# A decoder layer on one core: the output projection accumulates in the attention's four PSUM banks

## The chip, the cores and the metric

The kernel runs on one core of a Trainium2 chip (the profile calls it core 0 of [0]). The metric is the device time of one execution in microseconds (us). Three runs of the kernel before took 2811.61, 2813.51 and 2815.99 us; the median is 2813.51 us. The profile is of one further execution, which took 2810.97 us, with a traced span of 2809.2 us.

The engines are named as the profile names them: PE is the matrix engine, PEld its weight loads, DVE, ACT and POOL the three engines for vectors and scalars, SP the engine that issues the DMA transfers. Each runs its own instructions strictly in their order and waits on semaphores for the others.

## What is computed

One layer on 4096 tokens of width 1024. The input is normalised and projected into eight groups of 512 columns. Half of the columns feed eight heads of a dilated sliding-window attention with three patterns (dilations 16, 4 and 1), the other half four heads of a gated linear recurrence (HGRN2). Each branch is normalised per head and gated; both are put side by side, projected, added to the input, and normalised:

```python
y_attn = _head_rmsnorm(attn, attn_out_norm_w[layer], ATTN_HEADS) * jax.nn.silu(ag.astype(f32))
y_hgrn = _head_rmsnorm(rec, hgrn_out_norm_w[layer], HGRN_HEADS) * jax.nn.silu(hg.astype(f32))
mixed = jnp.concatenate([y_attn, y_hgrn], axis=-1).astype(x.dtype)
x = x + mixed @ w_out[layer]
...
return _rmsnorm(x, final_norm_w)
```

The change concerns `mixed @ w_out`: a 4096x1024 matrix times a 1024x1024 one, in float32.

## The kernel before

**Three stages.** The first (to about 720 us of the trace) makes the attention's projections for 32 blocks of 128 rows; it has its own PSUM pools, five banks `m` among them. The second (about 730 to 2360 us) interleaves the projections and the recurrence of the HGRN2 heads with the attention, which is a generator that yields after each piece and is advanced between the recurrence's blocks. The third (from about 2366 us) is the output projection. It overlaps the last pieces of the attention, since what `take(10 ** 9)` leaves of the generator is issued ahead of it.

**PSUM in the second and third stage.** Eight banks of 128x512 float32: one `proj` (pool `ps_p`), four `att` (`ps_t`), one `po` (`ps_o`), and `hp1` and `hp2` (`ps_h`). A tile of a pool with one bank can be written only when whoever reads the tile before it is done. A pool with four banks hands them out in the order of the program, so that a new tile waits for the readers of the fourth last one.

**Who uses them.** `project_T` and `project_N` of the HGRN2 heads use `proj`. The attention uses `att` for scores (`score`, L419 and L420), for transposed weights (`flip`, L442), for maxima and sums, and in `finish` for four tiles of transposed outputs (L599 and L600), which DVE multiplies into `pr` (L602). The output projection, `project`, uses `proj` as well.

**The output projection, row by row.** A row is a block `b` of 128 tokens. `load_y(b)` reads its two halves from DRAM into `raw` (three buffers, L870), transposes each with four matmuls into `hp1` and `hp2` (L874), and splits them into a high and a low part `xs` (ACT L170, DVE L171; five buffers). `project` then does 24 matmuls of 128x512 for each half `n` of the output columns: eight steps `k` of three products high x high (L183), high x low (L184) and low x high (L185). `residual` adds the bank to the input row `xr` on DVE (L904) and so frees the bank. `final_norm` takes the squares on ACT (L911), some small operations on DVE and ACT, and a scaling of the row on DVE (L914); the row is then written (L915). In the loop, `load_y(b + 1)` stands ahead of the two projections of `b`. The first two rows are apart: both are projected on the first half of the weights before the second half has been split (`w1hi`, `w1lo`, L862 and L863, from the four buffers `woraw`, L858).

**What sets the order.** The framework's scheduler orders each engine's instructions by a simulated timeline, so that the order in the program is not the order of the code; but the banks of a pool go round in the order of the code.

Of the kernel before, what the change touches and what calls it, by code (L numbers as in the profile page):

```python
# [17 lines left out]
F32 = mybir.dt.float32  # L18
# [31 lines left out]
def layer(ctx: ExitStack, tc: tile.TileContext, x, xT, xP, pos, w_in, w_out, nw, anw, hnw, lbraw, fnw,  # L50
# [124 lines left out]
        return t[:, 0:512], t[:, 512:1024]  # L175

    def project(X, W):
        ps = ps_p.tile([128, 512], F32, name="proj")
        for k in range(KT):
            hi, lo = X[k // 4]  # L180
            c = slice((k % 4) * 128, (k % 4 + 1) * 128)
            whi, wlo = W[k]
            T.matmul(ps, hi[:, c], whi, start=(k == 0), stop=False)  # L183
            T.matmul(ps, hi[:, c], wlo, start=False, stop=False)  # L184
            T.matmul(ps, lo[:, c], whi, start=False, stop=(k == KT - 1))  # L185
        return ps
# [626 lines left out]
    ps_p = ctx.enter_context(tc.tile_pool(name="ps_p", bufs=1, space=PSUM))  # L813
    ps_t = ctx.enter_context(tc.tile_pool(name="ps_t", bufs=4, space=PSUM))
# [72 lines left out]
    take(10 ** 9)  # L887
    Y = [load_y(0), load_y(1)]
    ps0 = [project(Y[0], WO[0]), project(Y[1], WO[0])]
    w1hi = big.tile([128, S], F32R, name="w1hi", tag="QS")  # L890
    w1lo = big.tile([128, S], F32R, name="w1lo", tag="KH")
# [27 lines left out]
    for b in range(2):  # L919
        residual(b, 1, project(Y[b], WO[1]))  # L920
        final_norm(b)
    Yn = load_y(2)
    for b in range(2, NB):
        Yb, Yn = Yn, load_y(b + 1) if b + 1 < NB else None
        for n in range(2):
            residual(b, n, project(Yb, WO[n]))
        final_norm(b)
# [50 lines left out]
```

## Time and profile before

| | |
|---|---|
| median of three runs | 2813.51 us |
| profiled execution, its own time | 2810.97 us |
| its span in the trace | 2809.2 us |
| PE busy | 2609.6 us (93%) |
| DVE, ACT, POOL busy | 1949.5 us (69%), 1714.1 us (61%), 917.1 us (33%) |
| DMA moved | 475.90 MB, mean 169 GB/s |
| first matmul of the output projection | at 2366.17 us |
| first matmul of row 2, where the loop begins | at 2406.76 us |
| last matmul | begins at 2799.52 us |

In the timeline a row gives start, duration, engine, line, operation, output and inputs, the number of merged instructions, and in brackets how long the engine had been idle and what ended that. Matmuls overlap, so the step from one start to the next is the time that each takes of PE; the duration of one is longer. In the table of stretches (windows), each stretch has the busy time of the engines with the number of instructions, the clock granted to PE (1.00 is full speed), the DMA engines' busy share and their rate. In the list of waits, each row gives who waited for whom, the sum in us, how often, and the longest.

### The profile page before, as it was taken

The page shows a single profiled execution, that of the slowest core. Times are in us where ns is not written, and L with a number is a line of the kernel's source. Part 1 is how long each engine was busy: PE and PEld are TensorE (multiplying, and loading weights), DVE is VectorE, ACT ScalarE, POOL GpSimd, SP SyncE. Part 2 cuts the span into 40 slices and gives each one's busy share as a digit, 9 for nine tenths or more (in the row PEclk, how much of TensorE's full clock was granted, in tenths as well). Part 3 has the DMA queues.
Part 4 walks back from the last instruction along what each step waited for, and adds up shares of the span by engine and source line. Part 5 has one row for each costly group of instructions (what it writes and reads, how often), then busy time and mean ns, then how long its engine had stood idle before and what let it go on. Part 6 is the DMA issues. An engine that isn't in the chain of part 4 may idle for free.

```text
span 2809.2 us, 52085 instructions
## 1 busy us (share of the span) xinstructions
PE 2609.6 (93%) x17330; PEld 2337.8 (83%) x17330; DVE 1949.5 (69%) x5267; ACT 1714.1 (61%) x4847; POOL 917.1 (33%) x900
## 2 busy tenths in 40 slices
PE   6899989999879999999999999999999998999997
PEld 4678867888769898899999899999899998777776
DVE  8777788777556786886777876777877768533343
ACT  8755565555557687677677786687776776222221
POOL 5456546565423453331331321422312312100000
PEclk8999999999989999999999999999999999999999
DMA  6855464444865865865756746647647545434432
GB/s 231 254 172 152 140 189 143 143 147 135 247 174 182 239 202 165 241 172 149 197 152 178 230 124 191 182 145 215 192 128 221 155 136 171 143 117 122 122 117 64
DMA packets 452192, 475.90 MB, mean 169 GB/s; under 512 B 119336, under 2 KB 334420, under 8 KB 451924
## 3 DMA queue, kind: packets, MB, share of 16 engines
q1 hardware_dynamic: 451924, 472.58, 56.9%
q8 instruction: 138, 2.26, 0.3%
q14 instruction: 130, 1.06, 0.1%
HBM read 346.06 MB, written 126.37 MB: 168 GB/s over the span
## 4 chain that ended last, share of the span: by engine, by line
PE 69%; DVE 13%; DMA 9%; ACT 4%; issue 2%; SPq 2%; POOL 1%; DVEq 0%; POOLq 0%; ACTq 0%
PE proj L210 19%; PE m L721 6%; PE m L719 6%; PE m L720 6%; PE po L454 5%; PE proj L183 5%; PE att L442 4%; PE proj L185 4%; PE proj L184 4%; PE att L419 3%; PE att L420 3%; DVE xr L904 2%; DMA y_d<-pr 1%; DMA raw<-x 1%; DMA mr<-ml_d 1%
## 5 line engine op out<-in xcount | busy, mean ns | idle before, releaser
L210 PE MATMUL proj<-xs,whi 128*128 128x256 f32 x2048 | 430.9, 299 | 10.7 <-ACT hgv L344 5.8
L210 PE MATMUL proj<-whi,xs 128*128 128x256 f32 x2048 | 414.4, 291 | 16.0 <-DVE hz L317 15.7
L210 PEld LDWEIGHTS proj<-xs,whi 128*128 128x128 f32 x2048 | 336.8, 198 | 18.3 <-ACT hgv L344 8.0
L210 PEld LDWEIGHTS proj<-whi,xs 128*128 128x128 f32 x2048 | 330.4, 192 | 19.0 <-DVE hz L317 9.5
L430 DVE CUSTOM_DVE_ANT_0 pt<-att,mask 128x256 f32<-128x256 f32 (+1 forms) x768 | 269.1, 388 | 97.6 <-PE att L420 94.8
L210 PE MATMUL proj<-xs,wlo 128*128 128x256 f32 x1024 | 305.6, 298 | 4.5 <-DVE wlo L162 4.5
L210 PE MATMUL proj<-wlo,xs 128*128 128x256 f32 x1024 | 295.4, 289 | 0.0
L446 DVE TENSOR_TENSOR pl<-att,ph 128x512 fp32r<-128x512 f32 (+1 forms) x384 | 237.4, 625 | 64.8 <-ACT ph L445 62.6
L432 ACT ACTIVATE pt<-pt,ml 128x256 f32<-128x256 f32 (+1 forms) x512 | 238.3, 468 | 45.3 <-DVE ml L430 44.2
L445 ACT ACTIVATE ph<-att 128x512 fp32r<-128x512 f32 (+1 forms) x384 | 203.2, 544 | 80.5 <-PE att L442 44.7
L442 PE MATMUL att<-ident,pt 128*128 128x128 f32 x1368 | 228.6, 279 | 4.3 <-ACT pt L432 2.5
L454 PE MATMUL po<-ph,vh 128*128 128x128 f32 (+1 forms) x856 | 212.6, 279 | 11.0 <-ACT ph L445 4.4
L210 PEld LDWEIGHTS proj<-xs,wlo 128*128 128x128 f32 x1024 | 201.7, 197 | 9.4 <-DVE wlo L162 6.7
L454 PE MATMUL po<-pl,vh 128*128 128x128 f32 (+1 forms) x856 | 204.6, 285 | 3.7 <-DVE pl L446 3.7
L210 PEld LDWEIGHTS proj<-wlo,xs 128*128 128x128 f32 x1024 | 197.1, 192 | 0.0
L454 PEld LDWEIGHTS po<-ph,vh 128*128 128x128 f32 x856 | 164.6, 192 | 15.8 <-ACT ph L445 4.9
L442 PEld LDWEIGHTS att<-ident,pt 128*128 128x128 f32 x1368 | 161.9, 143 | 9.9 <-ACT pt L432 3.5
L719 PE MATMUL m<-tw,ss 128*128 128x512 f32 x384 | 154.6, 403 | 16.0 <-ACT tw L170 6.6
L454 PEld LDWEIGHTS po<-pl,vh 128*128 128x128 f32 x856 | 164.7, 192 | 5.7 <-DVE pl L446 4.9
L419 PE MATMUL att<-KH,qc 128*128 128x256 f32 (+1 forms) x512 | 144.2, 306 | 15.6 <-DMA vh<-v_d 14.1
L720 PE MATMUL m<-tw,ss 128*128 128x512 f32 x384 | 153.9, 401 | 4.9 <-DVE tw L171 4.9
L721 PE MATMUL m<-tw,ss 128*128 128x512 f32 x384 | 155.1, 404 | 0.0
(256 smaller groups left out, 7502.3 us busy)
## 6 DMA issues: line engine op xcount, KB each, us to landing
xs<-xh_d SPq DMA_DIRECT2D x192, 512.0 KB
xr<-xT SPq DMA_DIRECT2D x128, 256.0 KB
qk_d<-stk SPq DMA_DIRECT2D x128, 256.0 KB
xh_d<-xs SPq DMA_DIRECT2D x64, 512.0 KB
vh<-v_d SPq DMA_DIRECT2D x512, 64.0 KB
raw<-x SPq DMA_DIRECT2D x64, 256.0 KB
v_d<-hl SPq DMA_DIRECT2D x128, 128.0 KB
raw<-xP SPq DMA_DIRECT2D x64, 256.0 KB
```

The costliest lines, as they stand in the source:

```text
L183: T.matmul(ps, hi[:, c], whi, start=(k == 0), stop=False)
L210: m = T.matmul(o, l, r, start=first is None, stop=(k == KT - 1 and g == len(groups) - 1 and n == 2))
L419: T.matmul(o, q[:, j % 2 * 128 : (j % 2 + 1) * 128], cols(KH, *ks), start=True, stop=False)
L430: V.tensor_tensor_reduce(out=p_, in0=o, in1=mask[:, (1, 4, 16).index(d), 256 - 128 * nk : 256], scale=-0.125, scalar=3e38, op0=ALU.add, op ...
L432: A.activation(p_, p_, AF.Exp, scale=-1.0, bias=m, accum_out=l)
L442: T.transpose(ps[:, n * 128 : (n + 1) * 128], loc[u], ident)
L445: A.activation(ph[:, :w], ps[:, :w], AF.Copy)
L446: V.tensor_sub(pl[:, :w], ps[:, :w], ph[:, :w].bitcast(F32))
L454: T.matmul(po[:, 128 * c : 128 * (c + n)], v, rh, start=(s == 0), stop=(s == len(steps) - 1))
L719: T.matmul(ps, hi[:, c], whi, start=start and k == 0, stop=False, skip_group_check=not start)
L720: T.matmul(ps, hi[:, c], wlo, start=False, stop=False, skip_group_check=not start)
L721: T.matmul(ps, lo[:, c], whi, start=False, stop=(k == 3), skip_group_check=not start)
```

## The change

The output projection's accumulator is a tile of the pool `ps_t`, under the attention's name `att`, instead of a tile of `ps_p`. The projections of the HGRN2 heads stay in `proj`. No instruction is added or taken away and no tile changes its size.

```diff
     def project(X, W):
-        ps = ps_p.tile([128, 512], F32, name="proj")
+        ps = ps_t.tile([128, 512], F32, name="att")
         for k in range(KT):
             hi, lo = X[k // 4]
             c = slice((k % 4) * 128, (k % 4 + 1) * 128)
```

Up to the end of the second stage both programs are alike on all engines; POOL's order is the same throughout. After that the scheduler orders PE, ACT, DVE and SP anew. Three places are shown, with buffer numbers and with the semaphores that an instruction waits for.

**PE, in the loop over rows, between the two projections of one row.** Before (`proj_34864` is the first half of the columns, `proj_34891` the second; `hp1_35028` holds half of a later row):

```order
L185 MATMUL proj_34864<-whi_32231,xs_34770 128x512
L874 MATMUL hp1_35028<-ident_89,raw_35026 128x128 [waits DMAHW2_49,DVE_49,PE_49]
L874 MATMUL hp1_35028<-ident_89,raw_35026 128x128 x3
L183 MATMUL proj_34891<-w1hi_32339,xs_34760 128x512 [waits DVE_49]
L184 MATMUL proj_34891<-w1lo_32340,xs_34760 128x512
```

Now the same boundary:

```order
L184 MATMUL att_34864<-wlo_32232,xs_34770 128x512
L185 MATMUL att_34864<-whi_32231,xs_34770 128x512
L183 MATMUL att_34891<-w1hi_32339,xs_34760 128x512
L184 MATMUL att_34891<-w1lo_32340,xs_34760 128x512
L185 MATMUL att_34891<-w1hi_32339,xs_34760 128x512
```

The transposes are gone from between the two projections, and the second one begins without a wait for DVE. The eight transposes of a later row stand together at the end of the row, ahead of the next row's first projection:

```order
L185 MATMUL att_34891<-w1hi_32339,xs_34770 128x512
L874 MATMUL hp1_34937<-ident_89,raw_34935 128x128 [waits DMAHW0_49,DVE_49]
L874 MATMUL hp1_34937<-ident_89,raw_34935 128x128 x3
L874 MATMUL hp2_34947<-ident_89,raw_34945 128x128 [waits DMAHW3_49,DVE_49]
L874 MATMUL hp2_34947<-ident_89,raw_34945 128x128 x3
L183 MATMUL att_34955<-whi_32189,xs_34851 128x512 [waits Activation_49]
```

That projection waits for ACT's copy of its own row (`xs_34851`), whose transposes stand one row earlier; it too has no wait for DVE.

**PE, at the end of the attention, before `finish` of the last eight blocks.** Before, the first projection (`proj_32289`) stood among the attention's instructions, behind the first two L600 of the last `finish` but one (`att_30206` and `att_30211`):

```order
L600 MATMUL att_30206<-ident_89,o1_29977 128x2x64
L600 MATMUL att_30211<-ident_89,o1_29977 128x2x64
L183 MATMUL proj_32289<-whi_32189,xs_32256 128x512 [waits Activation_49]
L184 MATMUL proj_32289<-wlo_32190,xs_32256 128x512
L874 MATMUL hp2_32261<-ident_89,raw_32259 128x128 [waits DMAHW1_49,Activation_49]
L874 MATMUL hp2_32261<-ident_89,raw_32259 128x128 x3
L874 MATMUL hp1_32271<-ident_89,raw_32269 128x128 [waits DMAHW3_49,DVE_49]
L874 MATMUL hp1_32271<-ident_89,raw_32269 128x128 x3
L185 MATMUL proj_32289<-whi_32189,xs_32256 128x512
L183 MATMUL proj_32289<-whi_32195,xs_32256 128x512
```

Now it stands behind all of the attention, after the last L600 of the last `finish`, and waits for DVE, which reads the bank `att_30376` (L602) four tiles earlier in the round:

```order
L600 MATMUL att_30376<-ident_89,o1_30320 128x2x64
L600 MATMUL att_30381<-ident_89,o1_30320 128x2x64
L874 MATMUL hp2_32470<-ident_89,raw_32468 128x128 [waits DMAHW4_49]
L874 MATMUL hp2_32470<-ident_89,raw_32468 128x128 x3
L874 MATMUL hp1_32480<-ident_89,raw_32478 128x128 [waits DMAHW5_49]
L874 MATMUL hp1_32480<-ident_89,raw_32478 128x128 x3
L600 MATMUL att_30386<-ident_89,o1_30320 128x2x64 [waits DVE_49]
L600 MATMUL att_30391<-ident_89,o1_30320 128x2x64
L183 MATMUL att_32289<-whi_32189,xs_32256 128x512 [waits DVE_49]
L184 MATMUL att_32289<-wlo_32190,xs_32256 128x512
```

The other three projections of rows 0 and 1 follow it directly. On DVE the four L602 of this last `finish` stand behind all eight L863, as they did before.

**ACT, at the same place.** One piece of the difference: rows with + are new here, rows without a sign stand in both.

```order
 L170 ACTIVATE xs_32286<-hp2_32281 128x512
+L445 ACTIVATE ph_30262<-att_30257 128x512
+L445 ACTIVATE ph_30305<-att_30300 128x512
+L432 ACTIVATE pt_30246,nat_27647<-pt_30246,nat_27647 128x256 x2
+L170 ACTIVATE xs_32465<-hp1_32460 128x512
+L445 ACTIVATE ph_30334<-att_30329 128x512
+L608 ACTIVATE pr_30205<-pr_30205 128x8x64
+L587 ACTIVATE wt_30367<-wt_30367 128x24
+L445 ACTIVATE ph_30342<-att_30338 128x384
+L460 ACTIVATE pot_30321<-po_30309 64x256
 L862 ACTIVATE w1hi_32339<-woraw_32239 128x512
 L862 ACTIVATE w1hi_32339<-woraw_32241 128x512
```

Before, the first two L862, which wait for a DMA, stood ahead of the attention's last L445 copies; now they stand behind them. On SP two loads of input rows (L902, 512 KB each) stand ahead of the first four loads of `woraw`, which they followed before.

## Prediction

> **What bounds the kernel now.** I read the page's head first, then the table of stretches, the list of waits over the loop, and the timeline of PE there.
>
> ```profile
> span 2809.2 us, 52085 instructions
> PE 2609.6 (93%) x17330; PEld 2337.8 (83%) x17330; DVE 1949.5 (69%) x5267; ACT 1714.1 (61%) x4847; POOL 917.1 (33%) x900
> ```
>
> PE is the bound, but over the whole span this says nothing about the last stage. The stretches do:
>
> ```profile
> 200.00:300.00 100.00, 100.00 (x461) 82.75 (x461) 75.36 (x131) 52.06 (x96) 60.00 (x50) 1.00 0.48 145
> 2380.00:2386.00 6.00, 5.97 (x25) 5.38 (x26) 5.81 (x14) 5.24 (x16) 0.00 (x0) 0.50 1.02 396
> 2500.00:2600.00 100.00, 94.16 (x428) 75.11 (x427) 37.16 (x83) 22.30 (x59) 0.00 (x0) 1.00 0.42 122
> ```
>
> In 2500 to 2600 us PE is busy 94.16 of 100 us at a clock of 1.00, DVE 37, ACT 22, and the DMA engines 42% at 122 GB/s, where they reached 396 GB/s in 2380 to 2386. So nothing but PE and what it waits for can set the pace. What it waits for, from row 2 (2406.7 us) to the end:
>
> ```profile
> PE proj L183 <- DVE xr L904: 25.8, 60, 0.9
> PEld proj L183 <- DVE xr L904: 20.2, 31, 1.2
> PEld proj L183 <- ACT xs L170: 17.5, 27, 0.6
> ```
>
> All 60 projections of the 30 rows wait for DVE to add the one bank to the input row. One row of PE's timeline:
>
> ```profile
> 2419.93 0.47 PE L183 MATMUL proj<-whi,xs 128*128 128x512 f32 x1 [0.44 <-DVE xr L904]
> ...
> 2425.50 0.60 PE L874 MATMUL hp<-ident,raw 128*128 128x128 f32 x4
> 2426.45 0.50 PE L183 MATMUL proj<-w1hi,xs 128*128 128x512 f32 x1 [0.35 <-DVE xr L904]
> ...
> 2430.66 0.39 PE L183 MATMUL proj<-w1hi,xs 128*128 128x512 f32 x1
> ...
> 2431.34 0.39 PE L183 MATMUL proj<-w1hi,xs 128*128 128x512 f32 x1
> ...
> 2432.02 0.60 PE L874 MATMUL hp<-ident,raw 128*128 128x128 f32 x4
> 2433.06 0.47 PE L183 MATMUL proj<-whi,xs 128*128 128x512 f32 x1 [0.44 <-DVE xr L904]
> ```
>
> A row takes 2433.06 - 2419.93 = 13.13 us. In it, three undisturbed matmuls take 2431.34 - 2430.66 = 0.68 us, so one takes 0.2267 and the 48 of a row 10.88. The other 2.25 us are eight transposes and what surrounds the two waits.
>
> **The change in the loop (a gain).** The order shows that the wait for DVE is gone at both boundaries and that the eight transposes now stand together. What they cost on a PE that does not stand still is not seen in the loop; the nearest rows are just ahead of it:
>
> ```profile
> 2366.72 1.03 PE L874 MATMUL hp<-ident,raw 128*128 128x128 f32 x8
> 2367.51 0.48 PE L185 MATMUL proj<-whi,xs 128*128 128x512 f32 x1
> 2367.83 0.40 PE L183 MATMUL proj<-whi,xs 128*128 128x512 f32 x1
> ...
> 2404.91 1.31 PE L874 MATMUL hp<-ident,raw 128*128 128x128 f32 x8
> 2406.76 0.50 PE L183 MATMUL proj<-whi,xs 128*128 128x512 f32 x1 [0.53 <-DVE xr L904]
> ...
> 2799.52 0.39 PE L185 MATMUL proj<-w1hi,xs 128*128 128x512 f32 x1
> ```
>
> Eight transposes take 2367.51 - 2366.72 = 0.79 us, and the step after them is 0.32 instead of 0.23, which is 0.09 more: 0.88 together. The other row has 1.31 for eight, but there the second four waited for DVE to empty their bank; in the new loop that copy has almost a whole row's time. I take 0.88 and keep 1.31 + 0.09 = 1.40 as the other end.
>
> From row 2 to the last matmul's end PE needed 2799.52 + 0.39 - 2406.76 = 393.15 us. Now it needs 30 x 10.88 = 326.4 us of projections and 28 x 0.88 = 24.6 us of transposes (those of rows 2 and 3 are done before), 0.16 us for the last matmul's own length: 351.2. The gain is 41.9 us, or 1.4 us in each of 30 rows; with 1.40 for the transposes it is 27.3. Nothing in this term can be a loss: no instruction is added. It holds only as long as DVE, ACT and the DMA engines keep up with a row of 10.88 + 0.88 = 11.76 us, and by the stretch above they are busy 37%, 22% and 42% of a longer one.
>
> **The change at the end of the attention (a loss).** Banks of `att` go round in the order of the code, and the projections come after the whole attention. So the first one, which began at 2366.17 us and filled PE while the attention waited for ACT and DVE, now waits for the first L602 of the last `finish`. The rows that decide when that is:
>
> ```profile
> 2371.49 1.94 DVE L602 TENSOR_TENSOR pr<-att,wt 128x384 f32<-128x384 f32 x4
> 2377.71 1.26 ACT L862 ACTIVATE w1hi<-woraw 128x512 fp32r<-128x512 f32 x2 [5.39 <-DMA woraw<-w_out]
> 2379.40 0.58 ACT L445 ACTIVATE ph<-att 128x512 fp32r<-128x512 f32 x1
> 2380.03 0.58 PE L454 MATMUL po<-ph,vh 128*128 128x256 f32 x1 [3.48 <-ACT ph L445]
> 2383.72 1.61 SPq L858 DMA_DIRECT2D woraw<-w_out  x2
> 2386.64 0.43 DVE L564 TENSOR_TENSOR o<-po,pot 64x256 f32<-64x256 f32 x1
> 2387.09 0.17 DVE L141 TENSOR_TENSOR nrr<-nrr,nrq 128x8 f32<-128x8 f32 x1
> 2388.53 1.63 POOL L614 TENSOR_TENSOR pr<-pr,sgt 128x512 f32<-128x512 f32 x1
> 2390.18 0.38 SPq L615 DMA_DIRECT2D y_d<-pr  x1
> 2391.45 0.63 ACT L862 ACTIVATE w1hi<-woraw 128x512 fp32r<-128x512 f32 x1 [2.13 <-DMA woraw<-w_out]
> 2391.54 0.28 PE L454 MATMUL po<-ph,vh 128*128 128x256 f32 x1
> 2394.57 0.43 DVE L564 TENSOR_TENSOR o<-po,pot 64x256 f32<-64x256 f32 x1
> 2395.03 1.02 DVE L602 TENSOR_TENSOR pr<-att,wt 128x384 f32<-128x384 f32 x2
> ```
>
> The attention itself gets faster. Before, ACT stood 5.39 us for `woraw` with L445 behind it, and PE then stood 3.48 us for L445. Now L445 can follow the transposes, which need banks freed by the four L602 from 2371.49 on (0.49 us each): after two of them, the scores and four transposes, some 2373.2 instead of 2379.40. From there to the last L564 it took 15.6 us (2395.0 - 2379.40), of which PE spent 2391.54 - (2386.64 + 0.43) = 4.5 us on a projection before it took up `po` again. Without it: 2373.2 + 11.1 = 2384.3.
>
> But L602 then waits for two more things. DVE has eight L863 ahead of it, behind ACT's L862, behind the loads of `woraw`. The first four now queue behind 1 MB of input rows, 2.5 us at 396 GB/s: about 2380.2 instead of 2377.7. L863 of these four frees the buffers at 2381 to 2384, and the last four land some 7.7 us after their issue, as before (issued at 2383.72, used at 2391.45): 2391.5, and with one L862 and one L863 about 2393. And `pr` has one buffer: its last content has to be in DRAM. L141 may come at about 2384.2 instead of 2387.09, POOL's two multiplications 3.1 us later (2388.53 + 1.63 - 2387.09), the write 3 to 5 us after that (issued at 2390.18, awaited by 2395.03): 2391. So the first projection begins at about 2393.3. It is no earlier than 2385, when the attention is done, and I put the late end at 2398, 3 us after L602 was done before.
>
> From there to row 2 PE has 96 matmuls (21.8 us) and four transposes (0.4). It will have stood idle for most of the 8 us before, and after the idle 3.48 us above it ran at a clock of 0.50 from 2380 to 2386: six such us cost 3; I take 2.5, with 0.7 and 3 as ends. Row 2 begins at 2393.3 + 22.2 + 2.5 = 2418.0 instead of 2406.76: a loss of 11.3 us; between 2385 + 22.2 + 0.7 = 2407.9 (1.1) and 2398 + 22.2 + 3 = 2423.2 (16.4).
>
> [...]
>
> **The sum.** 41.9 - 11.3 = 30.6 us. The profiled execution would have a span of 2809.2 - 30.6 = 2778.6 and a time of 2810.97 - 30.6 = 2780.4; it lies 2.5 us under the median, so the median becomes 2813.51 - 30.6 = 2782.9. By the bounds the gain is between 27.3 - 16.4 = 10.9 and 41.9 - 1.1 = 40.8: 2802.6 to 2772.7. What follows the last matmul (9.3 us to the end of the span) has the same instructions.
>
> **The rivals.**
>
> *The start costs little.* If the loads of `woraw` and the write of `pr` land early, the loss is about 3 us: 2813.51 - 38.9 = 2774.6. For it: the attention alone is done some 9 us before my start. Against it: all three of the waits behind it hang on DMA at its busiest (1.02 in 2380 to 2386).
>
> *The transposes stay dear.* Eight for 1.40 us: 27.3 - 11.3 = 16.0, 2797.5. For it: every group of four in the loop lies 0.60 us long in the trace. Against it: 0.60 contains the end of the last matmul's pipeline, which overlaps with what follows where nothing waits.
>
> *Slower: another wait takes the loop's place.* PE's weight loads already wait for ACT's L170, 17.5 us in 27 rows, 0.65 each. If at the start of each row ACT's copy came as late as L904 does now, a row would stay at 13.13, and the late start would be left: 2813.51 + 11.3 = 2824.8. It decides as soon as a row wins under 11.3 / 30 = 0.38 us. Against it: the copy's transposes now stand a whole row ahead of its use, and ACT is busy 22%. [...]
>
> *PE falls to half clock while it goes round four banks.* Each of the 1440 matmuls of the loop would take twice as long: 326 us more than forecast, 3109. The row 200 to 300 us, where five banks `m` go round at 1.00, speaks against it. [...]
>
> *The change does nothing,* because a projection still waits for its own bank's reader: 2813.5. The new order of instructions, which has no such wait, all but excludes it.
>
> **How the numbers follow.** Forecast 2783 with 0.58 (its own range 2777 to 2790); cheap start 0.15; dear transposes 0.17; slower through another wait 0.05; nothing 0.04; half clock 0.01. The range from 2773 to 2799 takes in the forecast, both neighbours and nearly all of the bounds, and leaves the last three out. A measurement of this kernel tells 0.2%, 5.6 us, from no change: faster 0.90 (the first three), within 0.2% 0.04, slower 0.06.
>
> **What would show it.** In the loop, PE's steps from row to row are 11.8 us, no row shows a wait of L183 for L904, and eight transposes stand in about 0.8 us: otherwise the first term is wrong. At the attention's end the first L183 on `att` begins near 2393 behind an idle PE and a clock of 0.50 for some us, with L602, L863 and the write of `pr` just ahead of it, and row 2 begins near 2418: otherwise the second is. A row that is released by ACT's `xs`, or by the loads of `raw`, would mean that the wait has only changed its name.

## The result and the profile after

The changed kernel takes 2784.48 us (median of four runs, 2780.06 to 2789.19). The kernel before took 2812.56 us in the four runs beside it (2809.24 to 2815.99). The ratio is 0.990, with a 95% interval of 0.988 to 0.9921: 28 us faster. The forecast was 2783 us with a range of 2773 to 2799.

The head of the page of the changed kernel, whose profiled execution took 2784.72 us:

```profile
span 2782.9 us, 52052 instructions
PE 2599.4 (93%) x17330; PEld 2343.0 (84%) x17330; DVE 1940.1 (70%) x5267; ACT 1706.3 (61%) x4847; POOL 916.1 (33%) x900
```

PE's share is 93% as before, so the page alone does not show where 26 us of span went. The stretches do; the columns are those of the table of stretches above:

```profile
2392.00:2396.00 4.00, 0.00 (x0) 0.00 (x0) 1.50 (x3) 2.10 (x4) 0.12 (x1) 0.88 1.09 364
2396.00:2400.00 4.00, 2.08 (x5) 1.70 (x6) 3.07 (x6) 0.40 (x1) 0.61 (x1) 0.50 0.55 140
2400.00:2420.00 20.00, 20.00 (x85) 16.45 (x85) 6.48 (x19) 4.61 (x13) 4.27 (x4) 0.95 0.06 13
2500.00:2600.00 100.00, 100.00 (x479) 83.59 (x478) 40.14 (x92) 23.54 (x68) 0.00 (x0) 1.00 0.44 133
```

In the loop (2500 to 2600) PE is now busy all 100 us instead of 94.16, and works on 479 matmuls instead of 428. At the end of the attention there is a hole instead: nothing on PE from 2392 to 2396, while the DMA engines are busy throughout, and then half clock.

**The loop.** The timeline of PE shows two rows and the last matmul:

```profile
2515.43 1.03 PE L874 MATMUL hp<-ident,raw 128*128 128x128 f32 x8
2516.22 0.48 PE L183 MATMUL att<-whi,xs 128*128 128x512 f32 x1
2517.00 0.39 PE L183 MATMUL att<-whi,xs 128*128 128x512 f32 x1
...
2527.20 1.03 PE L874 MATMUL hp<-ident,raw 128*128 128x128 f32 x8
...
2773.32 0.39 PE L185 MATMUL att<-w1hi,xs 128*128 128x512 f32 x1
```

A row takes 2527.20 - 2515.43 = 11.77 us instead of 13.13. The eight transposes take 2516.22 - 2515.43 = 0.79 us, and the three matmuls behind them 0.78 instead of 0.68. No row has a bracket: PE never stands still. The list of waits over the loop (2419 to 2773 us) says the same from the other side. PE is nowhere in it as the one that waits, and DVE now waits for PE, 60 times:

```profile
DVE xr L904 <- PE att L185: 183.4, 60, 4.8
...
ACT xs L170 <- PE hp L874: 127.5, 29, 4.4
```

**The start.** The timeline of all engines where the attention ends, in order of time, with the first row as a mark that both programs reach by the same instructions in the same order (the first L600 of the last `finish` but one):

```profile
2370.92 0.40 PE L600 MATMUL att<-ident,o 128*128 128x128 f32 x2
...
2390.86 1.26 POOL L614 TENSOR_TENSOR pr<-pr,sgt 128x512 f32<-128x512 f32 x1
2391.45 0.45 PE L600 MATMUL att<-ident,o 128*128 128x128 f32 x2
2392.15 0.38 SPq L615 DMA_DIRECT2D y_d<-pr  x1
2393.84 2.56 ACT L862 ACTIVATE w1hi<-woraw 128x512 fp32r<-128x512 f32 x4 [3.05 <-DMA woraw<-w_out]
2394.50 2.62 DVE L863 TENSOR_TENSOR w1lo<-woraw,w1hi 128x512 fp32r<-128x512 f32 x4 [3.26 <-ACT w1hi L862]
2397.30 1.95 DVE L602 TENSOR_TENSOR pr<-att,wt 128x384 f32<-128x384 f32 x4 [0.18 <-DMA y_d<-pr]
2397.92 0.79 PE L183 MATMUL att<-whi,xs 128*128 128x512 f32 x1 [6.01 <-DVE pr L602]
...
2401.88 0.39 PE L183 MATMUL att<-whi,xs 128*128 128x512 f32 x1
...
2421.96 0.48 PE L183 MATMUL att<-whi,xs 128*128 128x512 f32 x1
```

Read it from the bottom up. Row 2 begins at 2421.96. The first projection begins at 2397.92, after PE was idle for 6.01 us, released by L602. L602 came 0.18 us after the last L863, released by the write of `pr`, which had been issued at 2392.15. The attention itself was done on PE by 2391.90. Both holds on L602, the loads of `woraw` and the write of `pr`, end within 0.2 us of each other, so this trace cannot tell which of them matters.

**Two executions, one scale.** The kernel before reached the mark sooner:

```profile
2366.01 0.41 PE L600 MATMUL att<-ident,o 128*128 128x128 f32 x2
```

The difference, 4.91 us, arises ahead of anything that the change touches, so it is taken off when a time after is compared with a time before. What the change does lies in the stretch from the mark to the end of the span: 2809.2 - 2366.01 = 443.2 us before, 2782.9 - 2370.92 = 412.0 after, 31.2 us less.

### The profile page after: what moved, and what is told of

Read it like the earlier page. It is cut to its first block, busy times and chain, and to the rows that moved or that the text cites. A ratio compares the mean times of both kernels' runs of the same rounds, so it can differ in the third digit from the quotient of the medians.

```text
span 2782.9 us, 52052 instructions
## 1 busy us (share of the span) xinstructions
PE 2599.4 (93%) x17330; PEld 2343.0 (84%) x17330; DVE 1940.1 (70%) x5267; ACT 1706.3 (61%) x4847; POOL 916.1 (33%) x900
## 4 chain that ended last, share of the span: by engine, by line
PE 66%; DMA 12%; DVE 11%; ACT 4%; issue 3%; SPq 2%; POOL 2%; DVEq 0%; POOLq 0%; ACTq 0%
PE proj L210 17%; PE m L721 5%; PE m L719 5%; PE m L720 5%; PE po L454 5%; PE att L183 4%; PE att L184 4%; PE att L185 4%; PE att L442 4%; PE att L419 3%; PE att L420 2%; DMA y_d<-pr 1%; DMA mr<-ml_d 1%; DMA KL<-qk_d 1%; DMA raw<-x 1%
## 5 line engine op out<-in xcount | busy, mean ns | idle before, releaser
L445 ACT ACTIVATE ph<-att 128x512 fp32r<-128x512 f32 (+1 forms) x384 | 203.0, 544 | 80.9 <-PE att L442 45.1
L904 DVE TENSOR_TENSOR xr<-att,xr 128x512 f32<-128x512 f32 x64 | 44.3, 692 | 194.7 <-PE att L185 194.7
L719 PE MATMUL m<-tw,ss 128*128 128x512 f32 x384 | 155.2, 405 | 18.5 <-ACT tw L170 6.5
L720 PE MATMUL m<-tw,ss 128*128 128x512 f32 x384 | 154.6, 403 | 4.3 <-DVE tw L171 4.3
```

The source lines that it names most:

```text
L445: A.activation(ph[:, :w], ps[:, :w], AF.Copy)
L719: T.matmul(ps, hi[:, c], whi, start=start and k == 0, stop=False, skip_group_check=not start)
L720: T.matmul(ps, hi[:, c], wlo, start=False, stop=False, skip_group_check=not start)
```

## The experiments

Two theories had to be told apart at two places. In the loop: one bank shared by all projections costs 1.4 us a row (mine), or something else in the new order does. At the start: the first projection is late because of the loads of `woraw`, because of the write of `pr`, or because of the attention alone. The edits are against the changed kernel. All results are collected in the table at the end of this part; it counts from the mark, since single executions differ ahead of it.

### The first two projections back in `proj`

```diff
-    def project(X, W):
-        ps = ps_t.tile([128, 512], F32, name="att")
+    def project(X, W, four=True):
+        ps = ps_t.tile([128, 512], F32, name="att") if four else ps_p.tile([128, 512], F32, name="proj")
...
-    ps0 = [project(Y[0], WO[0]), project(Y[1], WO[0])]
+    ps0 = [project(Y[0], WO[0], False), project(Y[1], WO[0], False)]
```

> Only the two early projections (rows 0 and 1, first half of the columns) go back to the bank proj; all other projections stay in att. Measure: the time from the two L600 of the last finish but one (2366.01 us in the trace of before, 2370.92 in the trace of the change; the programs are the same up to there) to the end of the span. It is 443.2 us before and 412.0 with the change. Theory (the loop wins 41.4 us because it no longer waits for L904, and the start loses 10.3 us because the first projections no longer fill the attention's last pieces): the two early projections come back to about 0.2 and 19 us after the mark, row 2 begins 41 us after it as before, the loop keeps 11.8 us a row, and the stretch is 402 us; the median is near 2772. Rival A (the gain hangs on the order that the scheduler gives when all projections come late): no loss is won back, 412 us. Rival B (the two effects aren't apart): the loop's rows become longer again, 13.1 us.

Measured: 2776.44 us (2775.77 to 2776.67), ratio to before 0.9864 (0.9835 to 0.9894). PE's timeline:

```profile
2372.46 0.65 PE L600 MATMUL att<-ident,o 128*128 128x128 f32 x2
...
2400.27 0.44 PE L600 MATMUL att<-ident,o 128*128 128x128 f32 x2 [1.99 <-DVE o L564]
...
2413.46 0.60 PE L874 MATMUL hp<-ident,raw 128*128 128x128 f32 x4
2413.82 0.47 PE L183 MATMUL att<-whi,xs 128*128 128x512 f32 x1
...
2530.82 1.03 PE L874 MATMUL hp<-ident,raw 128*128 128x128 f32 x8
...
2542.59 1.03 PE L874 MATMUL hp<-ident,raw 128*128 128x128 f32 x8
```

The stretch is 2774.8 - 2372.46 = 402.3 us. A row is 2542.59 - 2530.82 = 11.77 us, as in the changed kernel, and row 2 begins 2413.82 - 2372.46 = 41.4 us after the mark instead of 51.0; before it was 40.8. So the loss at the start comes from the first two projections alone, and the loop keeps its gain without them: from row 2 to the end of the span it takes 361.0 us here, 360.9 in the changed kernel and 402.4 before.

### The loop back in `proj`

```diff
-            residual(b, n, project(Yb, WO[n]))
+            residual(b, n, project(Yb, WO[n], False))
```

> The converse: rows 0 and 1 are projected in att, the loop from row 2 on in proj. Theory: the loss alone is left. The loop's rows take 13.0 to 13.2 us and wait for L904 at each projection; the first projection of rows 0 and 1 begins some 27 us after the mark as with the change; since half a projection of row 2 can go ahead in proj, some 2.7 us of the 10.3 are won back. Stretch from the mark 443.2 + 7.6 = 451 us, median near 2820, slower than before. Rival (the gain comes from the eight transposes standing together, not from the bank): the rows stay near 11.8 us and the time near 2784.

Measured: 2824.53 us (2819.83 to 2834.23), ratio to before 1.0033 (1.0018 to 1.0048): slower than before. PE's timeline:

```profile
2367.07 0.65 PE L600 MATMUL att<-ident,o 128*128 128x128 f32 x2
...
2378.19 0.47 PE L183 MATMUL proj<-whi,xs 128*128 128x512 f32 x1
...
2393.74 0.80 PE L183 MATMUL att<-whi,xs 128*128 128x512 f32 x1 [7.47 <-DVE pr L602]
...
2418.54 0.48 PE L183 MATMUL proj<-whi,xs 128*128 128x512 f32 x1
...
2520.84 0.47 PE L183 MATMUL proj<-whi,xs 128*128 128x512 f32 x1 [0.44 <-DVE xr L904]
...
2527.36 0.50 PE L183 MATMUL proj<-w1hi,xs 128*128 128x512 f32 x1 [0.35 <-DVE xr L904]
...
2533.99 0.47 PE L183 MATMUL proj<-whi,xs 128*128 128x512 f32 x1 [0.44 <-DVE xr L904]
```

With the one bank the two waits for L904 are back in every row, and a row is 2533.99 - 2520.84 = 13.15 us. The eight transposes stand in two groups of four again, but that by itself costs next to nothing: where nothing waits, four take 2413.82 - 2413.46 = 0.36 us (in the run before this one), two groups therefore 0.72, and eight at once 0.79. So the gain does not come from the transposes standing together.

The start is as late as in the changed kernel: rows 0 and 1 are done, and PE goes on with row 2, 2418.54 - 2367.07 = 51.5 us after the mark, 10.7 later than before. This is the start term by itself, as the run before it was the loop term by itself. The stretch, 451.0 us, is only 7.8 longer than before, since PE needed 399.6 us from there to the end instead of 402.4. Nearly all of that is the half projection that was expected to go ahead: `proj` is free while rows 0 and 1 wait for `att`, and twelve matmuls of row 2's first projection ran there from 2378.19 to 2381.05. At 2418.54 PE takes up the other twelve. Row 4 began at 2442.08, 23.5 us later, and with 12 x 0.227 = 2.7 us these are the 2 x 13.13 us of rows 2 and 3.

### Two banks in turn

The early two in `proj`, and in the loop the first half of the columns in `proj`, the second in `att`:

```diff
-    ps0 = [project(Y[0], WO[0]), project(Y[1], WO[0])]
+    ps0 = [project(Y[0], WO[0], False), project(Y[1], WO[0], False)]
...
-            residual(b, n, project(Yb, WO[n]))
+            residual(b, n, project(Yb, WO[n], n == 1))
```

> The first half of the columns accumulates in proj in every row, the second half in att, so that two neighbouring projections never share a bank, and proj is one bank as before. Theory: a projection of 5.4 us in another bank is time enough for L904 (0.69 us and its semaphores), so two banks do what four do: 11.8 us a row, no wait of L183 for L904; with the early projections back in the attention's end the stretch from the mark is 400 to 403 us, median near 2771. Rival (the depth of four matters, since DVE and ACT come late now and then): rows between 11.8 and 13.1 us, with waits for L904 left.

Measured: 2772.31 us (2771.2 to 2773.43), ratio to before 0.985 (0.9826 to 0.9875). PE's timeline:

```profile
2373.57 0.65 PE L600 MATMUL att<-ident,o 128*128 128x128 f32 x2
...
2399.05 0.48 PE L183 MATMUL proj<-whi,xs 128*128 128x512 f32 x1
...
2401.91 0.38 PE L600 MATMUL att<-ident,o 128*128 128x128 f32 x2
...
2527.65 1.03 PE L874 MATMUL hp<-ident,raw 128*128 128x128 f32 x8
...
2539.42 1.03 PE L874 MATMUL hp<-ident,raw 128*128 128x128 f32 x8
```

A row is again 11.77 us. So it is not four banks that the loop needs, but a second one: L904 takes 0.69 us (44.3 us for 64 in the changed kernel's groups), and PE works on the other half's bank for 24 x 0.227 = 5.4 us meanwhile. The stretch is 398.0 us, 4.3 less than with the early two in `proj` alone, and 2 to 5 less than expected. Two things make up the 4.3. Between the last two pairs of L600, where the kernel of the first experiment stood idle for 1.99 us, PE now does half of row 2's first projection (2399.05 to 2401.91), since `proj` is free there and `att` is not: 12 x 0.227 = 2.7 us. And behind that idle time the kernel of the first experiment went on at half clock: its next eight matmuls took 2404.34 - 2400.86 = 3.5 us instead of 1.8. So it needed 2413.82 - 2400.86 = 13.0 us from the first matmul on `w1hi` to row 2, where this one needed 2413.42 - 2402.05 = 11.4: the other 1.6.

### Eight buffers for `woraw`

Now the two holds at the start. With eight buffers, no load waits for L863:

```diff
-    raws = [fetch_wo(1, k, fp, "woraw", 4) for k in range(4)]
+    raws = [fetch_wo(1, k, fp, "woraw", 8) for k in range(KT)]
...
-        raw = raws[k] if k < 4 else fetch_wo(1, k, fp, "woraw", 4)
+        raw = raws[k]
```

> The changed kernel with eight buffers for the raw second half of the weights in place of four, so that the last four loads no longer wait for L863. In the trace of the change the first L602 of the last finish began at 2397.30 us, 26.4 us after the mark (the two L600 of the last finish but one), behind two waits that ended together: L863, which waits for the loads, ended at 2397.12, and the write of pr to DRAM, which L602 waits for as well, landed just before 2397.3. Theory (both hold the start): with the loads early, the write still holds it, and the first L183 on att begins 25 to 27 us after the mark, the stretch from mark to end is 411 to 412 us. Rival (the loads alone hold it): 21 us after the mark, 407 us.

Measured: 2781.7 us in one run, stretch 411.85. PE, DVE and SP in the timeline:

```profile
2368.05 0.65 PE L600 MATMUL att<-ident,o 128*128 128x128 f32 x2
...
2390.11 0.38 SPq L615 DMA_DIRECT2D y_d<-pr  x1
2393.35 1.95 DVE L602 TENSOR_TENSOR pr<-att,wt 128x384 f32<-128x384 f32 x4 [4.20 <-DMA y_d<-pr]
2393.97 0.80 PE L183 MATMUL att<-whi,xs 128*128 128x512 f32 x1 [3.62 <-DVE pr L602]
```

All L863 were done by 2387.84. After two short L564 DVE stood idle for 4.20 us until the write of `pr` was done, and the first projection began 2393.97 - 2368.05 = 25.9 us after the mark, against 27.0. The write alone holds the start nearly as long as both. It was issued at 2390.11 and awaited until 2393.35, 3.2 us, where the changed kernel needed 5.15 (2392.15 to 2397.30) beside the loads of `woraw`. The DMA engines were busy in that time (1.09 from 2392 to 2396), but what made the write longer is not shown.

### The last products not into `pr`

The last `finish` writes its products over 1536 columns of `OA`, which is no longer needed there, so that L602 does not wait for the write:

```diff
-        pr = tp.tile([128, 8, 3, 64], F32, name="pr", bufs=1)
+        if h == NH - 1 and b0 == NB - 8:
+            pr = OA[:, 0:1536].rearrange("p (b d c) -> p b d c", d=3, c=64)
+        else:
+            pr = tp.tile([128, 8, 3, 64], F32, name="pr", bufs=1)
```

> The changed kernel, in which the last finish puts its products into columns of OA that are no longer read, so that its L602 does not wait for the write of the products before. Theory (both hold the start): the loads of woraw still hold it, the first L183 on att begins 26 to 27 us after the mark, the stretch is 411 to 412 us. Rival (the write alone holds it): 21 us after the mark, 407 us.

Measured: 2783.41 us in one run, stretch 2781.6 - 2376.10 = 405.5. PE and DVE in the timeline, where lines from here on are three higher (L603 was L600, L605 was L602, L866 was L863):

```profile
2376.10 0.41 PE L603 MATMUL att<-ident,o 128*128 128x128 f32 x2
...
2395.65 0.65 PE L603 MATMUL att<-ident,o 128*128 128x128 f32 x2
2396.12 1.02 DVE L605 TENSOR_TENSOR OA<-att,wt 128x384 f32<-128x384 f32 x2 [0.65 <-PE att L603]
2397.28 0.48 PE L183 MATMUL att<-whi,xs 128*128 128x512 f32 x1
2400.76 2.60 DVE L866 TENSOR_TENSOR w1lo<-woraw,w1hi 128x512 fp32r<-128x512 f32 x4 [2.42 <-ACT w1hi L865]
```

The expectation fell. The first projection began 2397.28 - 2376.10 = 21.2 us after the mark, not 26 to 27, although the loads of `woraw` were as late as ever: the last four L866 began at 2400.76, behind the projection's begin. The scheduler had put DVE's instructions in another order. In the changed kernel all eight L863 stand ahead of the four L602; here, in DVE's order, only four do (the last two of them and what follows, without the rows of other lines):

```
...
L866 TENSOR_TENSOR w1lo<-woraw,w1hi 128x512 x2
L605 TENSOR_TENSOR OA<-att,wt 128x2x192 x2
L866 TENSOR_TENSOR w1lo<-woraw,w1hi 128x512 x4
L605 TENSOR_TENSOR OA<-att,wt 128x2x192 x2
```

So the loads held L602 only through an order that was made with the write of `pr` in it. That they would hold it as long in the old order, without the write, was not tried: an edit that takes the wait away makes the order anew.

### Both edits

> Both edits, eight buffers and the other place for the products. Theory: now the attention itself sets the start, or the last L863: the first L183 on att begins 21 to 24 us after the mark, and the stretch is 406 to 409 us. Rival (something else holds the start, for instance DVE's order): 26 us and 411 us as with the change.

Measured: 2783.68 us in one run, stretch 2781.9 - 2373.26 = 408.6. PE's timeline:

```profile
2373.26 0.40 PE L603 MATMUL att<-ident,o 128*128 128x128 f32 x2
...
2394.66 0.80 PE L183 MATMUL att<-whi,xs 128*128 128x512 f32 x1 [1.16 <-DVE OA L605]
```

The first projection begins 21.4 us after the mark, as without the eight buffers. What is left is nearly all the attention itself: the L603 that the first L605 needs comes 2392.85 - 2373.26 = 19.6 us after the mark here and 2395.65 - 2376.10 = 19.6 there. (Here L605 began 0.55 us after that L603 was done, since DVE had L866 ahead of it up to 2394.01.) The stretch is 3.1 us longer than in the run before, since the projection here begins at half clock: its first 14 matmuls took 2400.76 - 2394.66 = 6.1 us instead of 3.2. There, transposes had filled the place of the idle 1.16 us, PE had worked without a gap from 2393.49, and the first matmul of the projection ran at full speed 3.8 us later.

### The time of the whole program

The single runs of the last three kernels, 2781.7 to 2783.7 us, tell nothing of a stretch that is up to 6.5 us shorter. So the kernel with the products over `OA`, the changed kernel and the two banks in turn were timed on one chip, with no further edit.

> The kernel in which the last finish writes its products over OA instead of pr, for the time of the whole program: in its single profiled execution the first projection started 21.2 us after the mark (2397.28 less 2376.10) instead of the 27.0 of the changed kernel (2397.92 less 2370.92), yet the program as a whole took 2783.4 us, next to 2784.5 for the changed kernel. Theory: the 6 us are won, and the single execution only happened to reach the mark late; the median is then about 2778 us. Rival: the other order of the instructions ahead of the mark costs what the earlier start wins; the median is then 2783 to 2785 us, the mark again near 2376.

> The changed kernel unchanged, beside the two others on the same chip: 2784 us if the times of one chip stand for another. Its mark says how far one execution differs from another ahead of the projection: 2370.92 us in its first profile, 2366.01 in that of the kernel before, with the same instructions in the same order up to there. If chance sets it, it comes out anywhere between 2365 and 2375; if the changed program itself sets it, near 2371 again.

> Early two in proj, in the loop the first half of the columns in proj and the second in att, again: 2771 to 2773 us, 12 to 13 us below the changed kernel on the same chip, if what it wins is the start of the stretch (10.3 us) and half a projection of row 2 ahead of the loop (a few us).

Measured: 2775.41 us (2766.87 to 2780.75) for the products over `OA`, 2781.96 (2773.59 to 2785.23) for the changed kernel, 2764.71 (2758.09 to 2768.49) for the two banks, beside 2813.28 us before; the ratios to before are 0.9865 (0.9841 to 0.9888), 0.9881 (0.9859 to 0.9903) and 0.9827 (0.9809 to 0.9845).

The products over `OA` win 6.5 us on the median and 412.3 - 405.65 = 6.7 us in the stretch, so the earlier start is not paid back elsewhere; this median is 2.6 us under the 2778 expected, and the spread of its four runs is wider than that. The two banks win 17.2 us on the changed kernel where 12 to 13 were expected; the stretch explains 412.3 - 398.7 = 13.6 of them, and the rest lies within the spread of the runs. On the mark, the changed kernel alone decides nothing (2371.18, near its first 2370.92). But the kernel with the two banks reached it at 2363.12 and, in its earlier profile, at 2373.57:

```profile
2363.12 0.41 PE L600 MATMUL att<-ident,o 128*128 128x128 f32 x2
```

One and the same program differs by 10.4 us there from one execution to another (the two were on different chips; whether the chip or the execution makes the difference was not tried).

| kernel | span | mark | mark to end | first projection of row 0 after the mark | median | before, beside it |
|---|---|---|---|---|---|---|
| before | 2809.2 | 2366.01 | 443.2 | 0.2 | 2812.56 | |
| changed | 2782.9 | 2370.92 | 412.0 | 27.0 | 2784.48 | 2812.56 |
| changed, again | 2783.5 | 2371.18 | 412.3 | 26.4 | 2781.96 | 2813.28 |
| first two in `proj` | 2774.8 | 2372.46 | 402.3 | 0.3 | 2776.44 | 2817.38 |
| loop in `proj` | 2818.1 | 2367.07 | 451.0 | 26.7 | 2824.53 | 2817.38 |
| two banks in turn | 2771.6 | 2373.57 | 398.0 | 0.3 | 2772.31 | 2817.38 |
| two banks, again | 2761.8 | 2363.12 | 398.7 | 0.2 | 2764.71 | 2813.28 |
| eight `woraw` | 2779.9 | 2368.05 | 411.9 | 25.9 | 2781.7, one run | 2815.92, one run |
| products over `OA` | 2781.6 | 2376.10 | 405.5 | 21.2 | 2783.41, one run | 2815.92, one run |
| the same, again | 2779.0 | 2373.35 | 405.7 | 21.1 | 2775.41 | 2813.28 |
| both | 2781.9 | 2373.26 | 408.6 | 21.4 | 2783.68, one run | 2815.92, one run |

## Why the prediction was right

**The loop term was right in mechanism and size.** Forecast were 11.76 us a row and 351.2 us from row 2 to the last matmul's end; measured are 11.77 and 2773.32 + 0.39 - 2421.96 = 351.75. The gain is 41.4 us (41.9 forecast). The transposes cost 0.79 + 0.10, where 0.79 + 0.09 were taken from a row ahead of the loop. The choice of that row over the 1.31 of the other one was the largest single choice in the sum, 14.6 us, and it was the right one for the reason given: no copy is waited for any more. Put back by itself, the one bank restores 13.15 us a row and both waits.

**The start term was right in size; one of its two reasons was not independent.** In the scale of before, 4.91 us taken off, the first projection began at 2393.01 (2393.3 forecast) and row 2 at 2417.05 (2418.0). The loss is 10.3 us (11.3 forecast); by itself it is 10.7, in the run with the loop in `proj`, where half a projection of row 2 then wins 2.7 of it back. The chain's steps:

- The last L862 and L863, behind the loads, were done at 2397.12 - 4.91 = 2392.2 (about 2393 forecast).
- The write of `pr` was done by 2392.4 (2391 forecast). POOL ended at 2392.12 - 4.91 = 2387.2, just as forecast, but the write then took 5.2 us, at the long end of the 3 to 5.
- That L602 waits for both is true of the changed kernel's order. But that the loads are a hold of their own, as the forecast had it, is not shown: without the write, the order changes and they stop mattering; without the loads, the write holds nearly as long. Whether the loads alone would hold in the old order stays open.
- The attention alone was done later than thought: its last L564 ended at 2391.25 - 4.91 = 2386.3, not 2384.3. Hidden behind the holds this cost nothing. It is most of the reason why taking the holds away wins 6 us of start and not the 8.3 between 2385 and 2393.3.
- The half clock cost 1.9 us, not 2.5: the first nine matmuls took 2401.88 - 2397.92 = 3.96 us, where 3 x 0.68 = 2.04 would be full speed. But in the run with the loop in `proj`, whose start is as late, twelve such matmuls took 2399.02 - 2393.74 = 5.28 us instead of 2.72: 2.56 us. So 2.5 lies within what these two starts show, and that row 2 came within 1 us of the forecast is in part luck.

**The sum.** 41.4 - 10.3 = 31.1 us, against 30.6 forecast and 31.2 in the stretch from the mark. On the medians the gain is smaller, 2812.56 - 2784.48 = 28.1 us, and the interval of the ratio leaves 22 to 34. The time itself came out at 2784.48, 1.5 us above the forecast; the profiled execution, 2784.72, is 4.3 above its 2780.4, by the 4.91 us that this execution was late ahead of the change.

**The rivals.** The cheap start (2774.6, 38.9 us less than before) did not happen, since L602 had to wait for the write of `pr`; made to happen, with the products over `OA`, it gives 2775.41 us, 37.9 less than before beside it. The dear transposes are excluded by the 0.79 us. No wait took the place of the one removed: the list of waits has no row with PE as the waiting engine, and ACT, which was to become late, itself waits for PE's transposes (127.5 us). The half clock while going round four banks is excluded by a clock of 1.00 from 2500 to 2600. Where only the start is changed, the kernel is slower than before (2824.53 us, beside 2817.38): the net gain rests on the loop alone.

## What to carry to other kernels

Before the change the loop's projections shared one PSUM bank with its reader, and PE waited for the reader, L904, at all 60 boundaries (25.8 us together). That cost 13.13 - 11.77 = 1.36 us for the two boundaries of a row, with eight transposes in between, and a second bank already takes all of it away (11.77 us a row with two banks, as with four). A pool that hands out its banks in the order of the code puts a second dependence on whoever else uses it: giving the loop the attention's banks was worth 41 us, giving them to the two projections that filled PE's gaps at the attention's end cost 10. So choose the bank for each use, the free one for work that is to run ahead, and compare executions from a mark behind which they differ.

## What was not expected of the hardware

The identical program reached the same instruction 10.4 us apart in two profiles (2363.12 and 2373.57), which is a third of what the change is worth; a difference of a few us between single spans says nothing.

Half clock came after a short gap too. In the first experiment PE was idle for 1.99 us, and the matmuls behind the gap came 0.43 us apart (2401.45 to 2404.01), where they had come 0.23 apart ahead of it (2393.14 to 2395.40). In the changed kernel a step of 0.43 goes with a clock of 0.50 (2398 to 2400).

The way back to full clock varied without any gap in the work: 3.8 us (products over `OA`), 4.0 (the changed kernel), 5.3 (loop in `proj`), and 6.5 in the second profile of the products over `OA`, where PE worked from 2390.24 on:

```profile
2390.24 0.55 PE L454 MATMUL po<-ph,vh 128*128 128x256 f32 x1 [3.02 <-issue]
...
2394.42 0.78 PE L183 MATMUL att<-whi,xs 128*128 128x512 f32 x1
...
2396.70 0.42 PE L185 MATMUL att<-whi,xs 128*128 128x512 f32 x1
```

With both edits PE worked from 2390.68 on, stood idle for 1.16 us, and was at full speed only from about 2400.8. A table of stretches of that kernel:

```profile
2392.00:2394.00 2.00, 1.50 (x8) 1.09 (x7) 2.00 (x6) 1.40 (x3) 0.00 (x0) 0.50 0.99 357
...
2398.00:2400.00 2.00, 2.00 (x7) 1.52 (x6) 0.00 (x0) 0.00 (x0) 0.00 (x0) 0.50 0.71 145
2400.00:2402.00 2.00, 2.00 (x9) 1.63 (x8) 0.00 (x0) 0.00 (x0) 0.00 (x0) 0.83 0.56 125
```

Counted from 2390.68 the way back is 10.1 us, more than in any run without a gap; counted from 2394.66, behind the gap, it is 6.1, among the others. Whether the gap of 1.16 us made the difference was not tried by itself.
